# Second-half operands of a Hymba block: T2 and B21 split when they are made instead of at their load

## The chip, the cores and the metric

The kernel runs on one core of one Trainium2 chip. The metric is device time in microseconds (us) of the whole launch: a median of 2069.72 us over three runs (2069.54 to 2070.18). The engines are TensorE (PE for its matmuls, PEld for its weight loads), VectorE (DVE), ScalarE (ACT), GpSimd (POOL) and SyncE (SP), which issues all DMAs of this kernel from one queue.

## What is computed

One decoder layer over 2048 positions of width 1024, in float32:

```python
h = rmsnorm(x, norm1_g)
p_q, p_k, p_v, p_g, p_a, c_b, c_c, c_h = split(h @ w_in)
o_gla = rmsnorm(gla_chunked(q, k, v, log_a)) * silu(p_g)     # 4 heads, gated linear attention
o_conv = c_b * causal_depthwise_conv(c_c * c_h, conv_w)
x = x + concat([o_gla, o_conv]) @ w_out
h2 = rmsnorm(x, norm2_g)
x = x + (silu(h2 @ w_ffn_gate) * (h2 @ w_ffn_up)) @ w_ffn_down
return rmsnorm(x, norm_f_g)
```

The part that matters here is the input projection `h @ w_in`, and of that its second half: positions 1024 to 2047.

## The kernel before, in words

**Split products.** A float32 matmul is made of three faster ones. Each operand is split into a high part, rounded to the reduced format float32r, and a low part, the difference. ACT makes the high part and DVE the low part (`split`, lines 196 and 197), and `product_step` (lines 446 to 448) adds high x high, high x low and low x high in one PSUM bank.

**Units.** A projection is cut into units (`unit`). A unit is a 2 x 2 block product in Strassen-Winograd form: seven products instead of eight, each of 4 x 3 = 12 matmuls of 128 x 128 by 128 x 512, so 84 in all. Its weights come in one load of 1 MB into a `raw` tile (`raw_weights`, two buffers); POOL forms the sums (line 421), and ACT and DVE split the seven results into `wq` tiles (four buffers). Results leave PSUM by a copy on ACT (line 486) or an addition on DVE (line 475). The seven products and their operands are

```python
PRODUCTS = [
    ("A11", "B11"), ("S1", "T1"), ("S2", "T2"), ("A12", "B21"),
    ("S3", "T3"), ("S4", "B22"), ("A22", "T4"),
]
```

The right-hand names are the kinds of input operand. For each kind there are four tiles (k = 0 to 3), so a half needs 28 operand tiles. They fill the pool `op` (28 buffers, each a high and a low part of 128 x 512), so an operand of the second half can only be loaded when the last unit of the first half has done with the tile that it replaces.

**Two halves.** `in_proj(0)` works through ten units and the opening through two more for positions 0 to 1023; `in_proj(1)` does 12 units for the rest. While the first half runs on PE, `h1_ahead` makes the second half's operands in the background, one small step for every second product: it loads `xt` tiles, scales them (line 868) and lets POOL form the differences T1 to T4 (`combine`, lines 356 to 373). `put` then writes each operand to DRAM (the tensors `siB..` and `siT..`). A kind that is in the tuple `WHOLE_H1` is stored whole, 256 KB, and is split after its load; any other is split at once into tiles `hi` and `lo` and both are stored, 512 KB.

**Handover.** Between the halves `load_pairs` loads the 28 tiles in the order of `PRODUCTS`: whole kinds by `load_whole`, which loads into the low part and splits there (ACT, then DVE, in the trace `op<-op`), the others by `load_pair`. At the same time runs `gla_half(0)`, the gated linear attention of the first half, in chunks of 128 positions, again as background steps: its loads (`kq`, `ee`, `vt`, `gt`, 14 of 64 KB for a chunk), small matmuls (`sc`, `kt_ps`, `v_ps`, `o_ps`, `kv`, `ot`) and stores `sgla`. The convolution's results are stored as `sm`.

**What sets the order.** Every engine and SP's DMA queue work strictly in the order of their own instruction lists. A scheduler fixed that order when the program was built, from its own estimate of times, and it moves instructions of the background steps and of later units between those around them. Since a change in any step shifts these estimates, the diff's few lines alter the order of all five lists over some 150 us of the run.

Of the kernel before, what the change touches and what calls it, by code (L numbers as in the profile page):

```python
# [11 lines left out]
F32 = mybir.dt.float32  # L12
# [8 lines left out]
P = 128  # L21
D = 1024
SEQ = 2048
PB = 512
# [12 lines left out]
# [4 lines that stand above are left out]
# [3 lines left out]


WHOLE = ("T3", "B22", "T4")


WHOLE_H1 = ("T2", "B21") + WHOLE


C_G1, C_G2, C_GF, C_BG, C_GN, C_CW = 0, 8, 16, 24, 26, 27
# [4 lines left out]
def tile_hymba_block(ctx, tc, x, xt, win, wa, wgu, wout, wffn, wdown, wdown_first, small, out):  # L57
# [3 lines left out]
    def pool_of(name, bufs, **kw):  # L61
        return ctx.enter_context(tc.tile_pool(name=name, bufs=bufs, **kw))
# [8 lines left out]
    dram = pool_of("dram", 1, space=DRAM)  # L71
# [37 lines left out]
            [dram.tile([P, PB], F32, name=f"{name}{b}_{i}") for i in range(n)] for b in range(NB)  # L109
        ]  # L110

    def made_ahead(name, n, whole=WHOLE):
        return dram.tile([P, PB] if n in whole else [P, 2, PB], F32, name=name)

    s_kq, s_d, s_v, s_g = scratch("sk", 4), scratch("sd", 2), scratch("sv", 4), scratch("sg", 4)
    s_x1 = scratch("sx", KD)
# [3 lines left out]
        [  # L120
            {
                n: made_ahead(f"sa{half}_{m}_{n}", n)
                for n in ("B11", "B12", "B21", "B22", "T1", "T2", "T3", "T4")
            }
# [5 lines left out]

    s_h2p = {
        n: [made_ahead(f"sh{n}_{k}", n) for k in range(4)] for _, n in PRODUCTS
    }
    s_h1 = {
        n: [made_ahead(f"si{n}_{k}", n, WHOLE_H1) for k in range(4)] for _, n in PRODUCTS
    }

    def col(c):
# [14 lines left out]
    def store(dst, src):  # L153
        return nc.sync.dma_start(dst, src)
# [38 lines left out]
    def split(src, hi, lo):  # L193
        if ordered:
            return split_in_order(src, hi, lo)
        last_hi[:] = [act.activation(hi, src, AF.Copy)]  # L196
        last_lo[:] = [dve.tensor_tensor(lo, src, hi.bitcast(F32), ALU.subtract)]  # L197
        return last_lo[0]
# [116 lines left out]
    def no_operands():  # L315
        return {b: [] for _, b in PRODUCTS}

    def combine(src, g, rb, put):


        order = [kj for k in range(4) for kj in ((k, 0), (k, 1), (k + 4, 1), (k + 4, 0))]
        ahead, made = deque(), deque()

        def fetch():
            if order:
                k, j = order.pop(0)
                h = bt("h")
                load(h[:], src(k, j))
                ahead.append((k, j, h))

        def quad():
            k, j, h = ahead.popleft()
            fetch()
            with behind(last_plus if with_marks else []):
                return scaled(col(g + k), rb[j], h)

        def keep(*args):
            made.append(args)
            if not with_marks:
                put(*made.popleft())  # L340

        def kept():
            while made:
                with behind(last_out + last_plus):
                    put(*made.popleft())

        fetch()
        fetch()
        for k in range(4):
            kept()  # L350
            b11 = quad()
            keep("B11", k, b11)
            yield
            kept()
            b12, t1 = quad(), bt("t1")
            pool.tensor_tensor(t1[:], b12[:], b11[:], ALU.subtract)
            keep("T1", k, t1)
            yield
            kept()
            b22 = quad()  # L360
            pool.tensor_tensor(t1[:], b22[:], t1[:], ALU.subtract)
            keep("T2", k, t1)
            yield
            kept()
            pool.tensor_tensor(b12[:], b22[:], b12[:], ALU.subtract)
            keep("T3", k, b12)
            yield
            kept()
            b21 = quad()
            keep("B21", k, b21)  # L370
            yield
            kept()
            pool.tensor_tensor(t1[:], b21[:], t1[:], ALU.subtract)
            keep("T4", k, t1)
            yield
            kept()
            keep("B22", k, b22)
            yield
        kept()
# [174 lines left out]
    def rows_rstd(ssq, rb):  # L554

        v, l, y = [mtiny.tile([P, PT], F32, name=n, tag=n) for n in ("msq", "rl", "ry")]
        dve.tensor_scalar(v[:], ssq, 1.0 / D, EPS, ALU.mult, ALU.add)
        rsqrt_by_exponent(v[:], l[:], y[:])
        rep = bt("rep", (P, PT, P))
        for t in range(PT):  # L560
            dve.tensor_copy(rep[:, t, :], y[:, t : t + 1].to_broadcast([P, P]))
        yield
        rb.append(bank("rb_ps"))
        for t in range(PT):
            pe.transpose(rb[0][:, t * P : (t + 1) * P], rep[:, t, :], ident[:])
        yield
# [319 lines left out]
    def h1_ahead():  # L886

        def put(n, k, h):
            if n in WHOLE_H1:
                store(s_h1[n][k][:], h[:])  # L890
                return
            hi, lo = [bx[0].tile([P, PB], F32R, name=e, tag="b") for e in ("hi", "lo")]
            split(h[:], hi[:], lo[:])
            for e, y in enumerate((hi, lo)):
                store(s_h1[n][k][:, e, :], y[:].bitcast(F32))

        for b in (2, 3):
            rb = []
            yield from rows_rstd(squares[b][:, :, 0], rb)
            rbs[b] = rb[0]  # L900
        yield from combine(lambda k, j: xt[2 + j, :, k, :], C_G1, (rbs[2], rbs[3]), put)

    def load_pairs(src):
        ops = no_operands()
        for _, n in PRODUCTS:
            ops[n] = [(load_whole if n in WHOLE_H1 else load_pair)(p) for p in src[n]]
        return ops

    def load_whole(src):
# [581 lines left out]
    ops, raw, between, steps, rest = opening()  # L1491
# [6 lines left out]
    in_proj(0, ops, raw, between, rest)  # L1498
    drain_background(lambda: len(background) < 2)
    ops = load_pairs(s_h1)  # L1500
    background.append(gate(1, ops))
    in_proj(1, ops)
# [120 lines left out]
```

## Time and profile before

| | |
|---|---|
| median of 3 runs | 2069.72 us |
| the profiled execution's own time | 2068.42 us |
| span of the profile, from the first to the last instruction | 2066.7 us |
| PE, DVE, ACT, POOL busy | 98%, 69%, 47%, 41% |
| DMA | 418.35 MB, mean 202 GB/s |
| granted TensorE clock, mean | 0.997 |

In the profile's rows times are in us from the start of the span. A row of the timeline gives start, duration, engine, line of the kernel, operation, output <- inputs, size and count; in brackets stand the idle time of the engine just before it and what ended that. A row of the groups gives the count, then busy time and the mean in ns of one, then idle time. A row of the stretches gives busy time and number of instructions of each engine. The profile names the tiles of a pool by what they are used for, without buffer numbers.

Where the work of this document lies: from about 145 to 250 us the second half's operands are made; from about 255 to 310 us is the handover; `in_proj(1)` begins at about 275 us.

### The profile page before, as it was taken

Reading aid. Unit: us, or ns where it says so; the run is one execution under the profiler, and the core shown is the slowest. Engines: PE = TensorE matmul, PEld = TensorE weight load, DVE = VectorE, ACT = ScalarE, POOL = GpSimd, SP = SyncE. Lnnn points to the kernel's source line nnn. Section 1 sums busy time; section 2 is a strip of 40 time slices with the busy share of each in tenths; the row PEclk is TensorE's granted clock in tenths of the full one; section 3 lists DMA queues with packets and bytes.
Section 4 is the critical chain, followed back from the end, with each engine's and each line's share of the span. In section 5 each row is a group of like instructions: output and inputs, shape, how many; then the busy total and the mean of one; then the engine's idle time right before and its main releaser. Section 6 shows DMA issues by size and latency. Waiting matters only on the chain.

```text
span 2066.7 us, 27155 instructions
## 1 busy us (share of the span) xinstructions
PE 2023.0 (98%) x9271; PEld 1661.5 (80%) x9271; DVE 1426.3 (69%) x2137; ACT 965.7 (47%) x1928; POOL 842.0 (41%) x614
## 2 busy tenths in 40 slices
PE   9999989999999999999999999999999999999997
PEld 8778768878888888888888888787888878878786
DVE  7877886568752776677676577776766666667774
ACT  6754465666542344444444452334434443453344
POOL 0044422222102474464464345534644554434544
PEclk9999999999999999999999999999999999999998
DMA  7355694434597773555444576576444444486653
GB/s 260 123 193 182 211 334 157 134 112 151 178 315 284 260 270 123 179 193 193 172 175 163 213 278 243 184 280 274 154 178 163 165 151 168 171 310 224 237 215 126
DMA packets 188587, 418.35 MB, mean 202 GB/s; under 512 B 19776, under 2 KB 65056, under 8 KB 178976
## 3 DMA queue, kind: packets, MB, share of 16 engines
q1 hardware_dynamic: 188448, 416.61, 56.9%
q8 instruction: 73, 1.20, 0.2%
q14 instruction: 66, 0.54, 0.1%
HBM read 273.93 MB, written 142.61 MB: 202 GB/s over the span
## 4 chain that ended last, share of the span: by engine, by line
PE 85%; DVE 7%; DMA 3%; ACT 2%; issue 2%; POOL 1%; SPq 0%; DVEq 0%; ACTq 0%; POOLq 0%
PE mm L446 23%; PE mm L448 23%; PE mm L447 23%; PE mm L1185 3%; PE mm L1186 3%; PE mm L1188 3%; DVE wq L197 2%; DVE op L197 1%; DMA op<-shT 1%; PE a_ps L944 1%; PE mm L730 1%; PE mm L732 1%; PE mm L731 1%; PE o_ps L1109 1%; PE o_ps L1111 1%
## 5 line engine op out<-in xcount | busy, mean ns | idle before, releaser
L446 PE MATMUL mm<-op,wq 128*128 128x512 f32 x2467 | 962.5, 393 | 19.0 <-ACT c L486 7.9
L447 PE MATMUL mm<-op,wq 128*128 128x512 f32 x2467 | 960.9, 390 | 1.5 <-DVE op L197 1.5
L448 PE MATMUL mm<-op,wq 128*128 128x512 f32 x2467 | 950.3, 390 | 5.1 <-DVE wq L197 4.9
L197 DVE TENSOR_TENSOR wq<-raw,wq 128x512 fp32r<-128x512 f32 (+2 forms) x612 | 501.7, 825 | 275.6 <-ACT wq L196 273.4
L196 ACT ACTIVATE wq<-raw 128x512 fp32r<-128x512 f32 (+2 forms) x612 | 356.1, 587 | 589.2 <-PE mm L448 451.4
L446 PEld LDWEIGHTS mm<-op,wq 128*128 128x128 f32 x2467 | 463.4, 188 | 123.2 <-ACT c L486 9.9
L448 PEld LDWEIGHTS mm<-op,wq 128*128 128x128 f32 x2467 | 463.5, 188 | 105.4 <-DVE wq L197 8.3
L447 PEld LDWEIGHTS mm<-op,wq 128*128 128x128 f32 x2467 | 463.6, 188 | 98.8 <-DVE op L197 4.4
L421 POOL TENSOR_TENSOR raw<-s,raw 128x512 f32<-128x512 f32 (+2 forms) x95 | 122.7, 1291 | 471.7 <-DVE wq L197 408.0
L421 POOL TENSOR_TENSOR raw<-raw 128x512 f32<-128x512 f32 (+2 forms) x190 | 253.4, 1339 | 137.5 <-DVE wq L197 132.3
L421 POOL TENSOR_TENSOR s<-raw 128x512 f32<-128x512 f32 (+2 forms) x95 | 124.7, 1312 | 307.5 <-DMA raw<-in_win_dram 109.4
L475 DVE TENSOR_TENSOR y<-mm,y 128x512 f32<-128x512 f32 x185 | 126.7, 686 | 84.6 <-PE mm L448 84.1
L475 DVE TENSOR_TENSOR c<-mm,c 128x512 f32<-128x512 f32 x196 | 134.3, 685 | 73.2 <-PE mm L448 70.9
L1167 POOL TENSOR_TENSOR ssx<-ssx,q 128x512 f32<-128x512 f32 x52 | 76.9, 1493 | 156.3 <-ACT q L1166 156.0
L486 ACT ACTIVATE c<-mm 128x512 f32<-128x512 f32 x198 | 115.8, 586 | 18.1 <-PE mm L448 15.2
L1185 PE MATMUL mm<-op,wq 128*128 128x512 f32 x256 | 100.5, 394 | 0.0
L1186 PE MATMUL mm<-op,wq 128*128 128x512 f32 x256 | 99.7, 389 | 0.0
L196 ACT ACTIVATE wq<-s 128x512 fp32r<-128x512 f32 (+2 forms) x96 | 56.2, 586 | 86.0 <-PE mm L448 82.1
L197 DVE TENSOR_TENSOR op<-op 128x512 fp32r<-128x512 f32 x102 | 82.2, 834 | 6.7 <-ACT op L196 6.7
L197 DVE TENSOR_TENSOR wq<-s,wq 128x512 fp32r<-128x512 f32 (+2 forms) x96 | 84.1, 876 | 3.6 <-ACT wq L196 2.9
L1188 PE MATMUL mm<-op,wq 128*128 128x512 f32 x256 | 79.7, 390 | 0.0
L1380 POOL TENSOR_TENSOR y<-x,y 128x512 f32<-128x512 f32 x32 | 52.0, 1624 | 45.8 <-DVE y L475 41.4
(228 smaller groups left out, 1835.3 us busy)
## 6 DMA issues: line engine op xcount, KB each, us to landing
raw<-in_wffn_dram SPq DMA_DIRECT2D x44, 1024.0 KB, 6.3
sa_B<-so SPq DMA_DIRECT2D x47, 512.0 KB, 4.3
op<-sa_B SPq DMA_DIRECT2D x47, 512.0 KB, 6.7
raw<-in_win_dram SPq DMA_DIRECT2D x22, 1024.0 KB, 5.3
sa_T<-so SPq DMA_DIRECT2D x44, 512.0 KB, 4.5
op<-sa_T SPq DMA_DIRECT2D x44, 512.0 KB, 6.7
raw<-in_wdown_dram SPq DMA_DIRECT2D x24, 768.0 KB, 5.8
sx<-y SPq DMA_DIRECT2D x48, 256.0 KB, 3.9
```

The source lines that it names most:

```text
L196: last_hi[:] = [act.activation(hi, src, AF.Copy)]
L197: last_lo[:] = [dve.tensor_tensor(lo, src, hi.bitcast(F32), ALU.subtract)]
L421: eng.tensor_tensor(*args)
L446: pe.matmul(o[:], wh, xh, start=first and k == 0, stop=False, skip_group_check=True)
L447: pe.matmul(o[:], wh, xl, start=False, stop=False, skip_group_check=True)
L448: return pe.matmul(o[:], wl, xh, start=False, stop=k == n - 1, skip_group_check=True)
L475: last_plus[:] = [dve.tensor_tensor(t[:], o[:], t[:], ALU.add)]
L486: last_out[:] = [act.activation(t[:], o[:], AF.Copy)]
L1167: pool.tensor_tensor(ssq[:], ssq[:], q[:], ALU.add)
L1185: pe.matmul(o[e, j][:], wh, m[:, 0, :], start=k == 0, stop=False)
L1186: pe.matmul(o[e, j][:], wh, m[:, 1, :], start=False, stop=False)
L1188: pe.matmul(o[e, j][:], wl, ops[k][j][:, 0, :], start=False, stop=k == KD - 1)
```

## The change

`WHOLE_H1` goes. The second half of the input projection then uses the same tuple as the rest of the kernel, `WHOLE = ("T3", "B22", "T4")`: T3, B22 and T4 are stored whole and split at their load as before; T2 and B21, eight tiles in all, are split into `hi` and `lo` where they are made, stored as a pair, and loaded as a pair.

```diff
-WHOLE_H1 = ("T2", "B21") + WHOLE
...
-    def made_ahead(name, n, whole=WHOLE):
-        return dram.tile([P, PB] if n in whole else [P, 2, PB], F32, name=name)
+    def made_ahead(name, n):
+        return dram.tile([P, PB] if n in WHOLE else [P, 2, PB], F32, name=name)
...
     s_h1 = {
-        n: [made_ahead(f"si{n}_{k}", n, WHOLE_H1) for k in range(4)] for _, n in PRODUCTS
+        n: [made_ahead(f"si{n}_{k}", n) for k in range(4)] for _, n in PRODUCTS
     }
...
     def h1_ahead():
         def put(n, k, h):
-            if n in WHOLE_H1:
+            if n in WHOLE:
                 store(s_h1[n][k][:], h[:])
                 return
...
     def load_pairs(src):
         ops = no_operands()
         for _, n in PRODUCTS:
-            ops[n] = [(load_whole if n in WHOLE_H1 else load_pair)(p) for p in src[n]]
+            ops[n] = [(load_whole if n in WHOLE else load_pair)(p) for p in src[n]]
         return ops
```

## The prediction

> **What bounds the kernel now.** I read the page first: how busy each engine is, and the chain that ended last.
>
> ```profile
> PE 2023.0 (98%) x9271; PEld 1661.5 (80%) x9271; DVE 1426.3 (69%) x2137; ACT 965.7 (47%) x1928; POOL 842.0 (41%) x614
> ...
> PE 85%; DVE 7%; DMA 3%; ACT 2%; issue 2%; POOL 1%; SPq 0%; DVEq 0%; ACTq 0%; POOLq 0%
> ```
>
> TensorE (PE) is the bound: 98% busy, and 85% of the chain is its own work. A change that leaves its matmuls alone can move the time only where PE waits. So the second view is the table of stretches around the code that the diff touches (columns: length, busy time and count of PE, PEld, DVE, ACT, POOL, then granted clock, DMA share, GB/s).
>
> ```profile
> 150.00:175.00 25.00, 25.00 (x112) 20.71 (x111) 11.34 (x17) 9.80 (x17) 14.69 (x10) 1.00 0.47 164
> 175.00:220.00 45.00, 41.47 (x182) 34.03 (x181) 44.44 (x54) 20.81 (x42) 22.56 (x14) 0.99 0.66 215
> 220.00:250.00 30.00, 30.00 (x127) 24.41 (x126) 20.07 (x27) 11.62 (x24) 14.86 (x10) 0.95 0.61 205
> ...
> 264.00:280.00 16.00, 12.84 (x63) 9.63 (x62) 14.59 (x24) 8.01 (x16) 3.90 (x3) 1.00 1.04 401
> 280.00:300.00 20.00, 18.47 (x91) 14.20 (x89) 19.21 (x29) 15.56 (x39) 5.54 (x5) 1.00 0.94 298
> 300.00:330.00 30.00, 26.97 (x155) 22.31 (x156) 21.55 (x43) 15.83 (x40) 9.39 (x7) 1.00 0.66 215
> ```
>
> From 150 to 250 us the second half's operands are made beside the first half's units. DVE has room before 175 (11.34 of 25 us) and after 220 (20.07 of 30), but between them it is full: 44.44 of 45. From 264 to 310 is the handover, in which the 28 operands are loaded and the whole ones split: DVE is full again and DMA too (share 1.04 and 0.94). The third view is PE's waits in both, by its timeline.
>
> ```profile
> 218.27 0.50 PE L446 MATMUL mm<-op,wq 128*128 128x512 f32 x1 [3.53 <-ACT c L486]
> ...
> 275.24 0.50 PE L446 MATMUL mm<-op,wq 128*128 128x512 f32 x1 [0.22 <-ACT wq L196]
> ...
> 278.91 0.50 PE L448 MATMUL mm<-op,wq 128*128 128x512 f32 x1 [2.94 <-DVE wq L197]
> ...
> 302.98 0.47 PE L446 MATMUL mm<-op,wq 128*128 128x512 f32 x1 [3.39 <-ACT ee L1073]
> ...
> 307.74 0.48 PE L446 MATMUL mm<-op,wq 128*128 128x512 f32 x1
> ```
>
> So the stretch costs PE 3.53 us and the handover about 6.5 us in these rows. At 307.74 the second unit of half 1 begins. I compare the two kernels at that point, since behind it the instruction order is nearly the same in both: what PE is late there, it is late at the end.
>
> **The change part by part.** *What moves.* T2 and B21, four tiles each, are split into high and low parts where they are made, not after their load. The operation counts stay: ACT's and DVE's splits of loaded tiles fall from 20 to 12 in this place and those into `hi` and `lo` rise from 8 to 16.
>
> ```profile
> L197 DVE TENSOR_TENSOR op<-op 128x512 fp32r<-128x512 f32 x20 | 15.0, 774 | 1.5 <-ACT op L196 1.5
> ...
> L196 ACT ACTIVATE op<-op 128x512 fp32r<-128x512 f32 x20 | 11.6, 619 | 0.0
> ...
> L197 DVE TENSOR_TENSOR lo<-t,hi 128x512 fp32r<-128x512 f32 x3 | 2.9, 976 | 0.5 <-ACT hi L196 0.3
> ...
> L197 DVE TENSOR_TENSOR lo<-h,hi 128x512 fp32r<-128x512 f32 x3 | 2.0, 679 | 0.0
> ```
>
> The handover loses 8 x 0.774 = 6.2 us of DVE and 8 x 0.619 = 5.0 of ACT. The making gains 4 x 0.976 + 4 x 0.679 = 6.6 us of DVE. Each moved tile is stored twice (256 KB more) and loaded at 512 KB instead of 256 KB, 2.1 MB more each way.
>
> *Making: +1.6 us.* In the changed kernel's instruction order, two of the eight `lo` come before 175, in DVE's idle time; two lie between 176 and 217; four come later, where 220 to 250 has 10 us to spare. The two in the full stretch are paid, for PE's wait at 218.27 ends through DVE: line 1033, then ACT's split of it, then ACT's copy of line 486, in that order in ACT's queue.
>
> ```profile
> 178.56 1.78 DVE L197 TENSOR_TENSOR wq<-raw,wq 128x512 fp32r<-128x512 f32 x1
> ...
> 216.39 0.68 DVE L1033 TENSOR_TENSOR c<-mm,c 128x512 f32<-128x512 f32 x1
> ```
>
> The mean of the six rows above is (2.9 + 2.0)/6 = 0.82, so 2 x 0.82 = 1.6. Ends: 0, if other work gives way, and 2 x 1.78 = 3.6, if both run as long as the split at 178.56. A gain is excluded, as nothing leaves this stretch. The Trainium skill ("SBUF — State Buffer", section "SBUF: two separate sides") says that VectorE and GpSimd share a port pair as an exclusive lock and that the later one blocks for the other's whole instruction. The same form at 0.68 and 1.78 agrees with it; by the rule both paid splits could meet a POOL operation, which is the upper end.
>
> *SP's queue: the operand loads start later, +5.2 us.* This speaks most against the change. SP issues in order. Now:
>
> ```profile
> 241.96 0.97 SPq L151 DMA_DIRECT2D ee<-sd  x2
> ...
> 247.86 1.86 SPq L151 DMA_DIRECT2D kq<-sk  x4
> ...
> 255.40 1.81 SPq L151 DMA_DIRECT2D op<-siB  x4
> 264.49 1.63 SPq L151 DMA_DIRECT2D raw<-in_win_dram  x2
> ...
> 298.18 0.36 SPq L151 DMA_DIRECT2D raw<-in_win_dram  x1
> ```
>
> In the changed order the store of the last B21 `lo` stands behind the first four `kq` loads, ahead of the other 24 loads of the first two chunks, and all operand loads stand behind those. That `lo` stands on DVE behind a line-475 addition, which needs its product from PE.
>
> ```profile
> 245.56 1.51 DVE L1074 TENSOR_TENSOR kq<-kq,ee 128x256 f32<-128x256 f32 x1
> ...
> 249.79 0.68 DVE L475 TENSOR_TENSOR c<-mm,c 128x512 f32<-128x512 f32 x1
> ```
>
> The addition began at 249.79; the `kq` operation (1.51) and its partner move behind it, a T2 `lo` comes ahead of it, so about 248.9, plus 0.5 of queue, and the `lo` ends near 249.4. Then 24 loads at 1.86/4 = 0.465 are 11.2 us: the first operand load goes at 260.6, not 255.40. With the 1.6 from above, 262.2. Queued behind it are all operand loads, the `sm` stores between them, and the next weights. Ends: 0, if `lo` comes as early as the `ee` loads now do (241.96), and +7.
>
> *The next weights.* Now two raw weight loads go at 264.49 for the first two units of half 1, and the third at 298.18. In the changed order the first goes before the chunk loads. That removes PE's waits at 275.24 and 278.91, as POOL's row shows their cause:
>
> ```profile
> 273.53 1.30 POOL L421 TENSOR_TENSOR s<-raw 128x512 f32<-128x512 f32 x1 [18.64 <-DMA raw<-in_win_dram]
> ```
>
> But the second now stands behind all operand loads and one more chunk. What the queue carries from the first operand load up to that weight load: 16 x 0.52 + 12 x 0.26 MB of operands, 2.1 of `sm`, 0.5 of `sgla`, 0.9 of chunk loads = 15.1 MB. Before it was, up to the load at 298.18, 8 x 0.52 + 20 x 0.26 + 2.1 of weights and the same rest: 15.1 too. So I give it the same 298.18 - 255.40 = 42.8 us, and the issue falls at 262.2 + 42.8 = 305.0. A load of that size lands after 5.3 us:
>
> ```profile
> raw<-in_win_dram SPq DMA_DIRECT2D x22, 1024.0 KB, 5.3
> ...
> 255.00:300.00 45.00, 40.31 (x200) 31.07 (x198) 40.83 (x66) 31.00 (x77) 9.44 (x7) 1.00 0.97 342
> ```
>
> At 310.3 ACT can split (0.62), DVE makes the low part (0.69), and the unit begins at about 311.0, with its third matmul 0.3 late: 311.0 + 0.3 - 307.74 = **+3.6 us**. The 342 GB/s row checks the size: 45 us x 342 = 15.4 MB. Ends: at 401 GB/s (264 to 280) the 15.1 MB take 37.7 us, -1.5 in place of +3.6; at 298 (280 to 300) 50.7 us, +11.5.
>
> *What goes.* All that PE wins in unit 0, the waits at 278.91 and 302.98 included, is then spent waiting for these weights. The wait at 302.98 ended with DVE's late additions, for which eight fewer splits help.
>
> *The clock: +1.8 us.* Such a wait is longer than 3.5 us. After the one that ended at 218.27:
>
> ```profile
> 220.00:225.00 5.00, 5.00 (x17) 3.94 (x17) 0.76 (x2) 1.12 (x2) 1.45 (x2) 0.73 0.98 349
> ...
> 221.39 0.63 PE L446 MATMUL mm<-op,wq 128*128 128x512 f32 x1
> 221.82 0.63 PE L447 MATMUL mm<-op,wq 128*128 128x512 f32 x1
> ```
>
> Granted clock 0.73, and matmuls started 0.43 apart where 25 us hold 112 of them, 0.22 apart; about nine such are 9 x 0.2 = 1.8 us. After the wait of 3.39 there is none (clock 1.00 from 300 to 330). Ends: 0 and 1.8. The Trainium skill ("TensorE: Matmul & The Clock Gate", "Part 1: The HAM clock gate") says that an idle window of about 3.4 us halves the clock for about as long; both rows agree. By it alone the cost would be, as an estimate, 3.4/2 = 1.7.
>
> Sum: +3.6 + 1.8 = **+5.4 us**. The profiled execution took 2068.42 (span 2066.7 and 1.7 around it), so 2073.8; it lies 1.3 under the median of the runs, 2069.72, so for a median **2075.1 us**. A measurement of this kernel can tell about 0.2%, 4.1 us, from no change.
>
> **The rivals.**
>
> *Cancelled (2071.3).* DVE is what holds the handover, weights come just in time, and only the making's 1.6 us are left. For it: DVE full at 264 to 300. Against: DMA is full too, and its queue starts later.
>
> *Faster (2063).* The operand loads start when they did, plus 1.6, so the second weight load lands at 255.4 + 1.6 + 42.8 + 5.3 = 305.1, or 300 at 401 GB/s. Then PE keeps the 6.5 us of the handover: 2069.72 - 6.5 = 2063.2. It decides at the store of the last B21 `lo`: from about 244 us for its issue the loads do not slip. For it: 6.2 us of DVE leave the place where PE waits. Against: that `lo` is behind an addition at 249.
>
> *Head of the line on ACT (2082).* The changed order puts the 12 splits of loaded tiles in one row on ACT, T4's last, and the exponentials of chunk 0 ahead of a weight split that the last unit needs. If loads are as slow as 298 GB/s, everything behind, the PSUM copies and the next weights' splits, waits: +11.5, so about 2081 to 2082. For it: ACT issues in order; against: the 342 mean.
>
> **How the numbers follow.** Forecast (late weights): 0.55, its own range 2071 to 2079, of which about 0.46 lies over +4.1 and 0.09 within. Cancelled 0.17 (0.15 within, 0.02 over). Faster 0.15. Head of the line 0.13. That makes slower 0.61, same 0.24, faster 0.15. The range for 8 in 10 leaves out most of the faster case and the tail of the slow one: 2066 to 2082.
>
> **What would show it.** Right: the first operand load issued near 262; a PE wait of several us for `wq` near 303 to 311, then some 3 us of a lower clock; no wait where 278.91 has one; DVE full a little longer past 217. Wrong: operand loads at 256, or weights of the second unit landing before unit 0 ends, by which the handover would be shorter than now; or a new wait before 250, which would put the cost into the making.

## The result, and the profile after

The changed kernel takes 2078.3 us (median of five runs, 2074.74 to 2079.52), the kernel before beside it 2069.72 (2068.43 to 2071.96). The ratio is **1.0033, with a 95% interval of 1.0021 to 1.0044**: slower by about 7 us (the two medians alone lie 8.6 apart). The profiled execution of after took 2079.07 us, 10.65 more than that of before, and that single pair is what the traces below compare. After's line numbers are smaller by three: its 443 to 445 are before's 446 to 448, its 1072 is 1075.

The page first, its line of busy time:

```profile
PE 2031.4 (98%) x9271; PEld 1667.7 (80%) x9271; DVE 1426.2 (69%) x2137; ACT 968.4 (47%) x1928; POOL 845.2 (41%) x614
```

PE has the same 9271 matmuls and is busy 8.4 us longer (2031.4 against 2023.0). So in this pair of executions most of the added time is not waiting: the same matmuls ran more slowly. DVE's total is unchanged, as the counts said.

PE's waits of after in the making and the handover, by its timeline:

```profile
219.35 0.80 PE L443 MATMUL mm<-op,wq 128*128 128x512 f32 x1 [4.14 <-ACT c L483]
...
258.61 0.72 PE L1082 MATMUL sc<-kq 64*128 64x128 f32 x8 [3.51 <-DVE kq L1072]
...
297.36 0.50 PE L444 MATMUL mm<-op,wq 128*128 128x512 f32 x1 [1.16 <-DVE op L194]
...
313.19 0.50 PE L443 MATMUL mm<-op,wq 128*128 128x512 f32 x1 [3.92 <-ACT wq L193]
...
413.10 0.50 PE L443 MATMUL mm<-op,wq 128*128 128x512 f32 x1 [0.65 <-DVE c L472]
```

The waits of before at 275.24, 278.91 and 302.98 are gone. In their place stand one at 258.61, for the first chunk's `kq`, and one at 313.19, for the weights of the second unit; a wait of 1.16 like that at 297.36 follows at 304.59. The wait of 0.65 at 413.10 is the same in both kernels (404.91 before), and a good landmark: up to there after has lost 8.2 us.

The stretches of after, cut at these waits (columns as in the prediction):

```profile
175.00:220.00 45.00, 40.85 (x178) 33.16 (x178) 44.35 (x55) 22.22 (x46) 23.90 (x15) 0.98 0.67 218
...
264.00:280.00 16.00, 16.00 (x87) 12.69 (x86) 9.96 (x22) 10.71 (x28) 1.60 (x1) 1.00 0.91 348
280.00:300.00 20.00, 18.84 (x96) 15.34 (x95) 15.13 (x28) 13.36 (x32) 1.80 (x1) 1.00 1.05 397
...
219.35:227.35 8.00, 8.00 (x23) 6.39 (x24) 4.79 (x7) 2.60 (x5) 2.22 (x2) 0.63 1.05 335
227.35:257.00 29.65, 27.75 (x123) 22.59 (x121) 24.07 (x30) 12.64 (x26) 17.43 (x12) 1.00 0.55 192
257.00:264.00 7.00, 5.39 (x25) 4.46 (x26) 6.67 (x11) 3.10 (x9) 0.94 (x1) 0.76 0.46 121
264.00:312.00 48.00, 42.93 (x223) 33.78 (x221) 32.59 (x62) 29.02 (x69) 3.40 (x2) 1.00 0.93 346
312.00:320.00 8.00, 6.81 (x34) 5.93 (x34) 6.36 (x7) 4.79 (x15) 4.48 (x3) 0.79 0.92 286
320.00:412.45 92.45, 92.45 (x499) 74.96 (x497) 53.52 (x106) 51.94 (x128) 22.74 (x16) 1.00 0.50 159
```

and of before, from its wait at 218.27 to its landmark:

```profile
218.27:224.27 6.00, 6.00 (x19) 4.81 (x20) 2.01 (x4) 2.07 (x4) 1.28 (x1) 0.72 1.01 338
224.27:404.26 179.99, 172.27 (x903) 139.27 (x902) 128.07 (x221) 103.03 (x251) 48.16 (x33) 1.00 0.63 209
```

DVE is still full where the operands are made (44.35 of 45 us) and no longer in the handover (9.96 of 16 and 15.13 of 20, before 14.59 and 19.21). The column to read is the granted clock, 1.00 in the long stretches of both. A stretch of 8 us at 0.63 does 8 x 0.37 = 2.96 us less work than at full speed. After loses 2.96 behind 219, 7 x 0.24 = 1.68 behind 258 and 8 x 0.21 = 1.68 behind 313: 6.3 us. Before loses 6 x 0.28 = 1.68, once. So of the 7.1 us between the two ends (193.10 against 185.99), **4.6 are half clock** and 2.1 are longer waits (3.51 + 1.16 + 1.16 + 3.92 = 9.75 against 7.67); 0.4 is left. Of the other 3.5 of the 10.65, 1.1 lie before 219, about 0.7 were not placed, and 10 x 0.17 = 1.7 are one more half clock, which this one execution of after had behind 474. Its wait there and its stretch:

```profile
474.00 0.84 PE L1082 MATMUL sc<-kq 64*128 64x128 f32 x8 [2.45 <-DVE kq L1072]
```

```profile
470.00:480.00 10.00, 7.55 (x35) 5.84 (x34) 6.86 (x16) 4.51 (x11) 1.66 (x1) 0.83 0.50 149
```

Before has the same wait without the lower clock:

```profile
465.77 0.71 PE L1085 MATMUL sc<-kq 64*128 64x128 f32 x8 [2.45 <-DVE kq L1075]
```

```profile
462.00:472.00 10.00, 7.55 (x42) 5.98 (x41) 7.23 (x16) 4.77 (x13) 1.66 (x1) 1.00 0.50 149
```

A single profile therefore carries an accident of about 1.7 us for each such place; the ratios over many runs do not.

The pair overstates the half clock. Over the whole run its granted clocks are 0.997 and 0.993, and 0.004 x 2070 = 8.3 us is what PE's busy time grew by. But 0.997 is rare for before: the 89 executions of it beside the experiments have 0.9940 in the mean, and 5 of them reach 0.997. After's five have 0.9926. By these means **half clock makes about 0.0014 x 2071 = 3 us of the loss of about 7** (1 to 5 with so few values of after); the rest of the pair's 8.3 is mostly a lucky execution of before.

Now SP's queue of after (the rows that answer to 239 to 298 of before):

```profile
248.23 2.40 SPq L148 DMA_DIRECT2D kq<-sk  x4
253.06 0.32 SPq L151 DMA_DIRECT2D siB<-lo  x1
253.43 0.92 SPq L148 DMA_DIRECT2D ee<-sd  x2
...
265.83 1.80 SPq L148 DMA_DIRECT2D op<-siB  x4
...
307.60 0.38 SPq L148 DMA_DIRECT2D raw<-in_win_dram  x1
```

and the other engines around the last B21 `lo`:

```profile
251.25 0.68 DVE L472 TENSOR_TENSOR c<-mm,c 128x512 f32<-128x512 f32 x1
251.85 1.18 DVE L194 TENSOR_TENSOR lo<-h,hi 128x512 fp32r<-128x512 f32 x1
252.96 1.77 DVE L1023 SCALAR_TENSOR_TENSOR c<-u,sml,c 128x512 f32<-128x512 f32 x1
...
255.92 0.68 DVE L194 TENSOR_TENSOR wq<-raw,wq 128x512 fp32r<-128x512 f32 x1
256.73 1.49 DVE L1071 TENSOR_TENSOR kq<-kq,ee 128x256 f32<-128x256 f32 x1
258.15 0.41 DVE L1072 SCALAR_TENSOR_TENSOR kq<-kq,ee 128x256 f32<-128x256 f32 x1
...
256.28 0.42 ACT L1069 ACTIVATE ee<-ee 128x256 f32<-128x256 f32 x1 [3.28 <-DMA ee<-sd]
```

The `lo` ends at 253.0, its store goes at 253.06, the `ee` loads at 253.43, ACT's exponentials wait 3.28 us for them, and the `kq` operations that ran at 245.56 before now run at 256.73. The scores' matmuls come right behind them, at 258.61. Two things release the first `kq` operation at almost the same time: the exponential ends at 256.70, and the weight split ahead of it on DVE at 256.60.

The `ee` loads go 11.5 us later than before's at 241.96. For 2.4 of that SP stands waiting for the `lo` (250.63 to 253.06). The rest is order: before issues its first `kq` load at 239.08, between the stores of k = 3, and after only behind the last but one of them, T4's at 247.84.

### The profile page after: what moved, and what is told of

Its sections match the earlier page's. It is cut to its first block, busy times and chain, and to the rows that moved or that the text cites. A ratio compares the mean times of both kernels' runs of the same rounds, so it can differ in the third digit from the quotient of the medians.

```text
span 2077.3 us, 27168 instructions
## 1 busy us (share of the span) xinstructions
PE 2031.4 (98%) x9271; PEld 1667.7 (80%) x9271; DVE 1426.2 (69%) x2137; ACT 968.4 (47%) x1928; POOL 845.2 (41%) x614
## 4 chain that ended last, share of the span: by engine, by line
PE 80%; DVE 8%; DMA 4%; ACT 3%; issue 2%; POOL 1%; SPq 1%; DVEq 0%; ACTq 0%; POOLq 0%
PE mm L443 23%; PE mm L445 23%; PE mm L444 23%; DVE wq L194 2%; PE mm L1182 2%; PE mm L1183 2%; PE mm L1185 2%; DVE op L194 1%; DMA op<-shT 1%; DMA op<-sa_T 1%; PE mm L727 1%; PE a_ps L941 1%; PE mm L729 1%; PE mm L728 1%; PE o_ps L1106 1%
## 5 line engine op out<-in xcount | busy, mean ns | idle before, releaser
L194 DVE TENSOR_TENSOR op<-op 128x512 fp32r<-128x512 f32 x94 | 76.4, 846 | 4.9 <-ACT op L193 4.8
L1291 DVE TENSOR_TENSOR c<-c,c 128x512 f32<-128x512 f32 x66 | 70.0, 1061 | 0.0
```

## The experiments

All the kernels below are edits of before or after; only after's own line numbers differ from before's. Times are medians; the ratio is to the kernel before, run beside them on the same chip. Waits, half clock and rest are those of one profile, from the end of the wait near 219 to the beginning of the landmark wait of 0.65 near 405: the sum of the bracketed waits in PE's timeline, the sum over 40 equal stretches of length x (1 - granted clock), and the length less both.

| kernel | us | ratio, 95% interval | waits | half clock | rest |
|---|---|---|---|---|---|
| before | 2069.7 to 2071.8 | 1 | 7.67 | 1.73 | 176.6 |
| after | 2078.30 | 1.0033 [1.0021, 1.0044] | 9.75 | 6.39 | 177.0 |
| only_t2 | 2070.56 | 0.9998 [0.9989, 1.0007] | 5.97 | 4.80 | 176.9 |
| only_b21 | 2076.32 | 1.0028 [1.0017, 1.0040] | 7.17 | 8.51 | 176.1 |
| after_w_early | 2077.77 | 1.0034 [1.0022, 1.0047] | 8.98 | 3.44 | 178.1 |
| before_w_early | 2066.06 | 0.9980 [0.9971, 0.9988] | 3.27 | 1.69 | 176.9 |
| after_k3_pool | 2076.84 | 1.0036 [1.0023, 1.0050] | 8.95 | 6.47 | 177.1 |
| after_lo_pool3 | 2074.37 | 1.0015 [1.0007, 1.0024] | 7.08 | 5.07 | 176.8 |
| after_no_lo | 2068.96 | 0.9995 [0.9986, 1.0004] | 6.18 | 1.71 | 176.1 |
| after_fill | 2077.65 | 1.0035 [1.0023, 1.0047] | 6.78 | 3.23 | 181.9 |
| only_b21_last | 2075.34 | 1.0022 [1.0013, 1.0032] | 8.56 | 3.39 | 175.8 |
| b21_last_whole | 2072.62 | 1.0005 [0.9996, 1.0014] | 8.19 | 5.12 | 175.8 |
| b21_last_whole_w_early | 2074.36 | 1.0015 [1.0006, 1.0024] | 6.86 | 5.10 | 176.2 |
| lo3_on_pool | 2076.01 | 1.0022 [1.0012, 1.0032] | 7.67 | 3.41 | 177.7 |

The last column tests this way of counting: apart from after_fill, which adds matmuls, PE's own work in this section is 175.8 to 178.1 us everywhere. What differs is waits and half clock. These three columns are of one execution, which took up to 4.6 us more (after_k3_pool) or 3.6 less (only_b21_last) than its kernel's median, so they show where time goes and the ratios how much. The row of before is the execution with the rare clock of 0.997, so its half clock is smaller than before's usual one.

My theory after the result was the prediction's, widened: the cost comes from SP's order, through late operand loads and late weights, and from the half clock behind each long wait. Its rivals were the number of splits and the number of bytes.

### Which of the two kinds: only_t2, only_b21

```diff
-WHOLE_H1 = ("T2", "B21") + WHOLE
+WHOLE_H1 = ("B21",) + WHOLE      # only_t2; only_b21 has ("T2",)
```

> T2 alone is split when it is made; B21 stays whole. Theory Queue (the cost comes from SP's order: a low part's store ahead of the chunk loads, and the second unit's weights behind all operand loads, each long PE wait then paying 1.7 us more at half clock): both places are still there, since the last T2 low part's store stands behind the first chunk load and two weight loads stand behind the last operand load, so most of the change's +6.8 us: 2074 to 2078. Rival Splits (the four extra low parts on DVE cost by their number) and rival Traffic (1 MB more each way costs by its size): half of it, about +3.4, 2073; under both, this run's and the next one's excess add up to the change's.

> B21 alone is split when it is made; T2 stays whole. Theory Queue: the late B21 low part's store stands again among the first chunk loads and the second unit's weights behind the operand loads and a chunk, so nearly the whole +6.8 us: 2075 to 2079. Rivals Splits and Traffic: half of it, 2073.

T2 alone costs nothing that shows (0.9998), B21 alone 1.0028, nearly the whole. The two do not share the cost by halves, so neither the number of splits nor the bytes sets it. My own theory expected most of it from T2 too and missed that. What it missed weighs against the prediction's own path as well, for only_t2 has both of its events, late operand loads and a wait for the second unit's weights:

```profile
261.80 2.42 SPq L151 DMA_DIRECT2D op<-siB  x4
...
303.23 0.85 SPq L151 DMA_DIRECT2D raw<-in_win_dram  x2
...
308.83 0.50 PE L446 MATMUL mm<-op,wq 128*128 128x512 f32 x1 [1.61 <-ACT wq L196]
```

The loads go 6.4 us later than in before, nearly the 6.8 of the forecast, and that costs nothing that shows. PE's row in only_b21 shows what only_t2 does not have (there 0.75 at 252.80), a long wait about where after has that at 258.61:

```profile
257.65 0.79 PE L446 MATMUL mm<-op,wq 128*128 128x512 f32 x1 [4.22 <-ACT c L486]
```

### The late weights: after_w_early, before_w_early

```diff
-    ops = load_pairs(s_h1)
+    raws = [raw_weights(win[u]) for u in range(2)]; ops = load_pairs(s_h1)
...
-    in_proj(1, ops)
+    in_proj(1, ops, raws)
...
-                yield unit(win[u], ops, eng=dve if (half, u) == (0, 3) else pool)
+                yield unit(win[u], ops, raw=raw[u] if half and u < 2 else None, eng=dve if (half, u) == (0, 3) else pool)
```

> The changed kernel, with the raw weights of the next half's first two units asked for ahead of the operand loads; the splits, the stores and the operand loads are as in the changed kernel. Theory Queue: the wait of 3.92 us for the second unit's weights goes, and with it about 1.7 us of half clock, while the operand loads come 1 MB later, so -3 to -5.5 us against the changed kernel: 2073 to 2075. Rivals Splits and Traffic: no change, 2078, as nothing is split or carried less.

> The kernel before, with the same two weight loads ahead of the operand loads. Theory Queue: the waits of 0.22 and 2.94 us for the first unit's weights go; the operand loads come 1 MB later, which takes back up to 2.6 us at 400 GB/s: 2067 to 2070. Rivals Splits and Traffic: no change, 2069.7.

In after_w_early the second unit's weights were asked for at 268.69, not 307.60, and the wait for them is gone. The time is what it was, 1.0034, where I had expected 2073 to 2075. PE now meets its operands instead, with nine waits of 0.23 to 0.71 us between 296 and 309, of which this is one:

```profile
300.27 0.50 PE L447 MATMUL mm<-op,wq 128*128 128x512 f32 x1 [0.71 <-DVE op L197]
```

So the weights were what came last in after; with them early the operands do, which now load behind 1 MB more. Nor is it the half clock that keeps the loss: the five executions of after_w_early all have a mean clock of 0.994, those of before beside them 0.9942. In the order of before the same edit gains 0.2% (0.9980): the waits of 2.94 and 3.39 us go, seven small ones of 0.23 to 0.82 come, and the sum of waits falls from 7.67 to 3.27. **before_w_early is faster than both kernels.**

### Where the last stores stand: after_k3_pool, after_lo_pool3

```diff
-                store(s_h1[n][k][:, e, :], y[:].bitcast(F32))
+                (pool.dma_start if (n, k, e) == ("B21", 3, 1) else store)(s_h1[n][k][:, e, :], y[:].bitcast(F32))
```

This is after_lo_pool3; after_k3_pool does the same for the high and low parts of T2 and B21 of k = 3 and for T4 of k = 3.

> The changed kernel; the five last operand stores (T2 and B21 of k = 3, high and low parts, and T4 of k = 3) are issued from GpSimd's queue instead of SP's, so that SP's chunk loads stand directly behind a weight load. Splits, bytes and loads are the same. Theory Queue: the first operand load goes at 255 to 258, not 265.8, the waits at 258.61 and 313.19 go, and the time comes back to 2066 to 2071. Rival Volume (the 2.1 MB more of operand loads set the handover, whenever it starts) and rival Splits: 2076 to 2080.

> The changed kernel; only one store, that of the last B21 low part, leaves SP's queue for GpSimd's. Theory Queue in the form of the prediction (this one store holds up the loads): the operand loads go 2.4 us earlier, from 265.8 to 263.4, since the store went at 253.06 and the loads ahead of it ended at 250.6; 2075 to 2077. Theory Queue in a wider form (all five last stores push the chunk loads back): the same small gain here, and the whole one only in the run beside this. Rivals Volume and Splits: 2077 to 2079.

Both came out otherwise than I expected. after_lo_pool3 did move the operand loads only 1.9 us (263.97 in place of 265.83), yet the ratio fell to 1.0015. The wait near 258 stayed:

```profile
258.39 1.23 PE L1085 MATMUL sc<-kq 64*128 64x128 f32 x8 [3.29 <-DVE kq L1075]
```

Its `ee` loads had gone at 250.91, and ACT's exponentials ran at 253.41; but the `kq` operations stand on DVE behind the `lo`, two convolution steps and two weight splits, and ran at 256.52. So this wait is held by DVE's order as much as by the loads. after_k3_pool moved the operand loads by 6 us (259.83) and gained nothing, 1.0036. The DMA issues took POOL's time, and beside POOL's issues and sums DVE ran slower:

```profile
247.89 3.06 DVE L1026 SCALAR_TENSOR_TENSOR c<-u,sml,c 128x512 f32<-128x512 f32 x1
...
246.72 0.55 POOL L895 DMA_DIRECT2D siT<-lo  x1
247.28 1.31 POOL L373 TENSOR_TENSOR t<-h,t 128x512 f32<-128x512 f32 x1
248.52 0.56 POOL L895 DMA_DIRECT2D siB<-hi  x1
249.10 1.30 POOL L421 TENSOR_TENSOR raw<-s,raw 128x512 f32<-128x512 f32 x1
...
260.30 1.22 PE L1085 MATMUL sc<-kq 64*128 64x128 f32 x8 [3.81 <-DVE kq L1075]
```

The convolution step of 0.83 us in after took 3.06 here, and the wait for `kq` grew to 3.81. This kernel says that an earlier start of the operand loads alone is not enough; it does not say what the loads alone are worth, since it slowed DVE at the same time.

### Bytes against splits: after_no_lo

```diff
-            hi, lo = [bx[0].tile([P, PB], F32R, name=e, tag="b") for e in ("hi", "lo")]
-            split(h[:], hi[:], lo[:])
+            hi, lo = [h, h] if n in ("T2", "B21") else [bx[0].tile([P, PB], F32R, name=e, tag="b") for e in ("hi", "lo")]
+            None if n in ("T2", "B21") else split(h[:], hi[:], lo[:])
```

> The changed kernel without its new splits: T2 and B21 are stored twice as they are, once in place of each part, and loaded as pairs, so no low part of these two kinds is made anywhere (16 operations less on DVE and ACT than either kernel makes for them; the products of T2 and B21 are another sum). SP's order then is that of the kernel before, with 2.1 MB more each way. Theory Queue: operand loads at 255 to 257, handover relieved of 8 splits, 2063 to 2068. Rival Volume: 2074 to 2078. Rival Splits: at or below before, 2063 to 2069, without telling it from Queue.

At 0.9995 the 2.1 MB more each way show no cost. Alone this run cannot exclude one, since DVE and ACT are spared eight operations each (DVE has 2129 in place of 2137), which might pay for it; with only_t2, half the bytes at 0.9998, and b21_last_whole below, seven eighths at 1.0005, rival Volume falls. But the time did not go down to 2063 to 2068 either, though the handover has eight splits fewer than in before and the operand loads start as early (255.83). PE meets the first unit's weights there:

```profile
278.39 0.50 PE L446 MATMUL mm<-op,wq 128*128 128x512 f32 x1 [3.99 <-ACT wq L196]
```

### The half clock: after_fill

```diff
+    filler = lambda o, m, n: [with_order(m, lambda: pe.matmul(o, ones[:], ones[:], start=True, stop=True)) for _ in range(n)]
...
-        sc = [ps.tile([P, 2, P], F32, name="sc", tag="mm") for _ in range(2)]
+        sc = [ps.tile([P, 2, P], F32, name="sc", tag="mm") for _ in range(2)]; filler(sc[0][:, 0, :], last_kq, 10 if t == 0 and b % 2 == 0 else 0)
...
-            o = bank() if first else o
+            o = bank() if first else o; filler(o[:, 0:P], first_hi, fills.pop() if fills and i == 0 else 0)
```

`with_order` only fixes the place in PE's list, and `fills` holds 12 for the second unit.

> The changed kernel with idle matmuls (128 x 128 of ones, into a bank that is overwritten next) in three of PE's waits: 10 ahead of the scores of the first chunk of each half, 12 ahead of the first product of the next half's second unit. Nothing waits less; PE only is not idle there. Theory Clock (a wait of 3.5 us costs 1.7 us more at half clock behind it): the half clock behind three waits goes, up to -5.1 us, 2073 to 2075. Rival (the half clock has another cause, or it costs nothing because the next wait swallows it): 2078 to 2080, the idle matmuls' own time.

The half clock was halved, from 6.39 to 3.23 us, and behind 258 it is gone:

```profile
255.00:264.00 9.00, 7.77 (x45) 6.42 (x45) 7.93 (x14) 5.28 (x13) 1.27 (x1) 1.00 0.47 118
```

The waits fell by 3.0 us. The idle matmuls themselves took 181.9 - 177.0 = 4.9 us, more than the waits that they were meant to fill, and the time stayed, 1.0035, where I had expected 2073 to 2075. So that the idle time at 258 causes the half clock behind it is shown; that its loss can be had back was not.

### One tile: only_b21_last, b21_last_whole, lo3_on_pool

In the orders of after, only_b21 and all kernels that kept the cost, one thing was common: the low part of B21, k = 3, the last part that is split before the handover. The next edits keep or move that tile alone.

```diff
+whole_h1 = lambda n, k: n in ("T2", "B21") + WHOLE and (n, k) != ("B21", 3)     # only_b21_last
+whole_h1 = lambda n, k: n in WHOLE or (n, k) == ("B21", 3)                      # b21_last_whole
...
-            if n in WHOLE:
+            if whole_h1(n, k):
...
-            ops[n] = [(load_whole if n in WHOLE else load_pair)(p) for p in src[n]]
+            ops[n] = [(load_whole if whole_h1(n, k) else load_pair)(p) for k, p in enumerate(src[n])]
```

> The kernel before, in which one tile alone, B21 of k = 3, is split when it is made. Theory One tile (what costs is the last B21 low part: its place in DVE's and SP's order pushes the first chunk's kq operations and the chunk loads behind it, PE waits 3.5 to 4.2 us near 258 us and pays about 1.7 us of half clock for each such wait): as the run with all four B21 tiles, ratio to before 1.0020 to 1.0035, 2075 to 2078, first operand load near 265. Rival Number (cost by the number of tiles split early): one eighth of +6.8, under 1.0005, 2071 to 2072.

> The changed kernel, in which that one tile, B21 of k = 3, stays whole; the other seven are split when they are made. Theory One tile: the first four kq loads and the kq operations come forward, no wait of over 3 us near 258, ratio 0.999 to 1.0005, 2069 to 2072. Rival Number: seven eighths of +6.8, ratio 1.0029, 2077.

Splitting this one tile early costs 1.0022 [1.0013, 1.0032]; splitting the other seven early and not this one, 1.0005 [0.9996, 1.0014], which is no measurable cost. **One tile of eight makes about two thirds of the whole loss** by the ratios; by their intervals it may be a third or all of it. The rows of only_b21_last show the way from SP to PE:

```profile
244.97 1.78 POOL L421 TENSOR_TENSOR raw<-s,raw 128x512 f32<-128x512 f32 x1 [3.82 <-DVE wq L197]
248.33 1.38 POOL L373 TENSOR_TENSOR t<-h,t 128x512 f32<-128x512 f32 x1 [1.59 <-DMA siT<-t]
...
243.51 0.32 SPq L154 DMA_DIRECT2D siB<-hi  x1
249.74 0.32 SPq L154 DMA_DIRECT2D siT<-t  x1
250.11 1.39 SPq L151 DMA_DIRECT2D kq<-sk  x3
251.60 0.38 SPq L154 DMA_DIRECT2D siB<-lo  x1
...
255.07 0.42 ACT L1072 ACTIVATE ee<-ee 128x256 f32<-128x256 f32 x1 [3.91 <-DMA ee<-sd]
256.36 0.58 ACT L486 ACTIVATE c<-mm 128x512 f32<-128x512 f32 x1
...
256.99 0.80 PE L446 MATMUL mm<-op,wq 128*128 128x512 f32 x1 [3.78 <-ACT c L486]
```

SP issues nothing from 243.8 to 249.74, where it waits for T4's difference. POOL makes that at 248.33, behind a weight sum that ran to 246.75 and 1.6 us more of idle time; in before it makes it at 243.81, ahead of that sum. The `ee` loads so go at 252.50, ACT's exponentials wait 3.91 us for them, and the copy out of PSUM that frees PE stands on ACT behind the exponentials. The same rows stand in only_b21 (T4's store at 250.21, exponentials at 255.73 behind 4.35 us for `ee`). So in these two kernels PE does not wait for `kq`, and the `lo` itself, done at 250.3, is on that way neither by its place on DVE nor by its store, which went with no wait as soon as three `kq` loads were issued. What the tile's split changed is the order around it.

In b21_last_whole the first `kq` load goes at 245.83 and the `kq` operations run at 254.82; PE's only wait there is 0.76 at 253.20. Later it has the events of the prediction: operand loads at 262.38, the second unit's weights asked for at 304.15, and a wait of 3.54 us for them at 310.01.

> The same, with the two weight loads of the next half ahead of the operand loads. If the early splits of the seven tiles relieve the handover, as the rival Faster of the prediction had it, then below the kernel before with the early weights: ratio under 0.9975, below 2066. If the handover is set by the operand loads and by the places of the splits on DVE and ACT, no better than it: ratio 0.998 to 0.9995, 2067 to 2070.

Ratio 1.0015, outside both ranges that I had given and slower than before_w_early (0.9980) by more than the intervals allow: the seven early splits do not relieve the handover. Its largest wait is 3.67 us for a `kq` at 308.54. The rival Faster has no support left. And what a tile costs depends on the order around it: these seven cost nothing measurable with the late weights and about 0.35% with the early ones, as much as all eight in after.

The last kernel makes that one low part on GpSimd:

```diff
-            split(h[:], hi[:], lo[:])
+            split(h[:], hi[:], lo[:]) if (n, k) != ("B21", 3) else [act.activation(hi[:], h[:], AF.Copy), pool.tensor_tensor(lo[:], h[:], hi[:].bitcast(F32), ALU.subtract)]
```

> The changed kernel; the low part of B21 of k = 3 is made on GpSimd in place of DVE, so that it is ready before DVE's addition at 251 and DVE has one operation less ahead of the first chunk's kq operations. Splits, bytes and queues of the stores are the same. Theory One tile, by DVE's order and the store that waits for it: the ee loads go near 250 to 251 in place of 253.4, the kq operations 2 us earlier, the wait near 258 falls below 2 us, and most of the cost goes: ratio 1.000 to 1.0015, 2071 to 2075. If only the number of bytes and stores of this tile matters: ratio 1.003, 2078, as the changed kernel.

The `ee` loads went at 251.37, the wait near 258 fell to 1.69 us, and the ratio only to 1.0022 [1.0012, 1.0032]: above the range that I had given, below after's median, and not told apart from it. Waits of 0.7 to 1.45 us came later in the handover. DVE did not win what it gave away: POOL's added operation (248.06 to 249.80) pushed its weight sum back, and this now lay beside a split on DVE that took 0.68 in after:

```profile
250.27 1.78 DVE L197 TENSOR_TENSOR wq<-s,wq 128x512 fp32r<-128x512 f32 x1
...
249.76 1.74 POOL L421 TENSOR_TENSOR raw<-s,raw 128x512 f32<-128x512 f32 x1
```

**What stays open.** In the order with the late weights one tile carries most of the loss: that is shown by only_b21_last and b21_last_whole. How is shown only in part. In only_b21 and only_b21_last the wait near 257 comes from T4's store, since POOL made T4 late. In after the `lo` does take part, as SP waits 2.4 us for it and DVE's order releases the `kq` operation as late as the loads do. Taking its store from SP's queue gave about half back (1.0015), making the part elsewhere about a third (1.0022); the intervals of both touch after's, and each also put work on POOL. That the order, and not the split's own work, costs in after too is the likelier reading. A kernel that keeps the split and before's order would decide it; none was tried.

## Why the prediction was right or wrong

The sign held and the size was near: +5.4 us forecast, a ratio of 1.0026, against 1.0033. The events of the sum came too, but two kernels have them and pay nothing, while a wait that the sum does not contain goes with the cost. That the number still came close is in part luck.

- **Making, +1.6.** Right in mechanism, too large in size: the wait near 218 grew from 3.53 to 4.14 us and ended 1.08 later. The 2.96 us of lower clock behind it, where before has 1.68, were chance: of the eight kernels with a wait of 4.14 to 4.19 us there, six lost 1.5 to 1.7 in the 8 us behind it, and only after and after_k3_pool about 3.
- **SP's queue, +5.2, first operand load at 262.2.** Right as an event, too small: it went at 265.83, 10.4 us later than before in place of 6.8 with the making. The `lo`'s store went at 253.06 and not at 251.0 (249.4 and the making's 1.6), as DVE operations ahead of it ran longer, line 1017 at 248.29 for 1.77 us where before had 0.68; and from that store to the first operand load it took 12.8 us, not 11.2.
- **Next weights, +3.6.** As an event it was right: the second load went 41.8 us behind the first operand load (42.8 assumed), at 307.60, and the unit began at 313.19 behind a wait of 3.92. As the cause it failed. only_t2 has the operand loads at 261.80 and a wait of 1.61 for these weights, b21_last_whole has 262.38 and 3.54, and they cost 0.9998 and 1.0005. With these weights early, after_w_early cost the same as after, 1.0034.
- **What it left out is the step that failed.** It moved "the `kq` operation and its partner" behind the addition to find the time of the `lo`, and never asked who waits for the chunk loads and for `kq`. PE does: in after for the scores of the first chunk, a new wait of 3.51 us at 258.61 with 1.68 of half clock behind it, in only_b21 and only_b21_last for a copy behind ACT's exponentials. The list of signs looked for a new wait only before 250. after_fill aside, which fills that wait, the kernels with 3.29 us or more there cost 1.0015 to 1.0036, those with under 0.8 us 0.9980 to 1.0015. It is not the whole: lo3_on_pool, with 1.69 us there, still cost 1.0022.
- **What goes.** The waits at 275.24, 278.91 and 302.98 went, and what PE won by that was spent on later waits, as forecast.
- **The clock, +1.8.** It was counted once, at the handover's end; the trace of after has it behind three waits there, 6.3 us in place of before's 1.68. By the mean clocks of the runs the change adds about 3 us (1 to 5) and not 4.6, so whether 1.8 was too small is not settled. The condition given, a wait over 3.5 us, is enough but not needed: 2.45 us at 474.00 had a half clock too. And "only where PE waits" was too narrow: PE's own 9271 matmuls took 8.4 us longer in this pair.
- **The rivals.** Cancelled: out, for the interval begins at 1.0021. Faster: out, in after_no_lo and b21_last_whole_w_early fewer splits in the handover gave no time back. Head of the line: its mechanism is there, at another place. The exponentials waited 3.28 us for a load at 256.28, not at the handover's end, and in only_b21 and only_b21_last the copy that PE needs stands behind them; the 11.5 us that it was priced at did not come.

## What to carry to other kernels

When a step moves to an earlier place, take each instruction that it pushes back on its engine or its queue, name the instruction that waits for that, and go on until PE is reached; the transfer that I followed was there, and cost nothing in two other kernels. A wait of PE of 2 to 4 us can cost 1.7 or 3.4 us more in clock, so count the long waits of a change and not only their length. Read the clock over many runs before you price it: one pair of traces gave 8.3 us here, the means of the runs about 3. And before work is taken out of a full stretch, look what is last behind it: here the weights, whose earlier load was worth 0.2% in the kernel before, while the splits moved for the same stretch were worth nothing.

## What the runs showed of the hardware that was not expected

**The half clock comes in portions and, behind shorter waits, by chance.** The losses behind single waits were 1.7 us or twice that; after's 2.96 is two portions, the first of which began during the wait. Between 145 and 515 us the fourteen traces have 22 waits of 3.5 us or more, and a half clock stands behind every one. The wait of 2.45 us near 470 (the rows at 474.00 and 465.77 above) had it in 7 of the 13 traces that have that wait. A wait of 1.92 to 1.94 us near 83 stands in all fourteen, long before the second half's operands are made, and had it in 6: in lo3_on_pool (first row), not in before (second row).

```profile
85.00:90.00 5.00, 5.00 (x16) 3.91 (x16) 4.02 (x8) 4.33 (x10) 0.00 (x0) 0.66 0.87 273
```

```profile
85.00:90.00 5.00, 5.00 (x24) 4.11 (x23) 3.49 (x6) 4.95 (x12) 0.42 (x1) 1.00 0.89 314
```

The Trainium skill ("TensorE: Matmul & The Clock Gate", "Part 1: The HAM clock gate") describes a window of about 3.4 us that runs freely, whatever the kernel does, and a lower clock after an idle one. The portion of 1.7 us, half of 3.4, and the element of chance agree with it, and so do the 22 long waits; that a whole window must be idle does not, as waits of 1.93 and 2.45 us were enough here.

**Beside GpSimd's sums and DMA issues together DVE took longest.** In after_k3_pool the convolution step took 3.06 us where after has 0.83; beside it lay two of POOL's operations with issues between them, and it ended 0.55 behind the second. Beside one sum of POOL's, 247.78 to 249.52, a DVE operation in after took 1.77 (248.29). The issues alone did not slow DVE: a split at 246.33 beside two of them, 246.00 to 247.27, took 0.69. Each issue is listed with 0.55 to 0.72 us of POOL.
